# Three constants of a kernel's own planner, and sixteen small stores gathered into two

## The chip, the cores and the metric

The kernel runs on one core of one Trainium2 chip. The time is device microseconds of one execution; a kernel's time is the median over its runs. A core has TensorE (PE; its weight loads are listed as PEld), VectorE (DVE), ScalarE (ACT), GpSimd (POOL) and SyncE (SP), each with an instruction stream of its own that it works off in order, and 16 DMA engines that SP feeds here.

## The reference

One streaming step of a hybrid encoder layer, for 2048 frames of a new stream (the prompt) and 64 frames of a running one (the sample), width 1024, all in float32.

```python
h = rmsnorm(x, norm1_w)
proj = h @ w_in                       # q,k,v (3 x 512), z (512), a, b (4 each), u_pool (512)
qkv, conv_new = causal_short_conv(qkv_pre, conv_prev, conv_w)   # width 4; keeps the last 3 rows
...                                   # gated delta rule, 4 heads of 128, chunks; state S
o_pool, pool_new = multiscale_pool(u_pool, pool_prev, pos0, pool_w, pool_scale)  # keeps 15 rows
x = x + concat([o_delta, o_pool]) @ w_out
h = rmsnorm(x, norm2_w)
x = x + (silu(h @ w_gate) * (h @ w_up)) @ w_down                # 2816 wide
return rmsnorm(x, normf_w), conv_new, s_new, pool_new           # for prompt and sample
```

The histories that are returned are small: conv_new is 3 rows of 1536 channels, pool_new 15 rows of 512, for the prompt and again for the sample.

## The kernel before, in words

**The work.** Activations lie with channels on the partitions and frames along the free axis. Each float32 product is made of three matmuls in fp32r: weights and activations are split into a high part (a cast by ACT) and the rest (a subtraction by DVE), and high x high, high x rest and rest x high are summed in PSUM.

The *mixer* runs over four blocks of 512 frames; the first also holds the sample's 64. Per block: norm, input projection (21 weight tiles `win`), convolution, the delta rule (chains called Front and Head), pooling, output projection (`wout`). In the first block the split weights are stored to DRAM (`wnd`, and `wod` for the output projection, 512 KB each) and later blocks load them back (tile `wsp`). The output x2d goes to DRAM.

The *FFN* runs over three blocks of 704 frames in two halves of 352. `gate_up` makes one of 22 groups of 128 hidden channels with seven products of four tiles each, by a Strassen scheme: sums of weights (S1 to S4) times sums of activations (T1 to T4) are accumulated in three PSUM banks x, y and z. One product is 12 matmuls of 352 columns. In between, ACT and DVE copy or add what a bank holds so far (`g1`, `u2`, `g2`, in the trace g and u), and a later product accumulates into the same bank. The last one, weights 22 by T4 (px<-hBT,ws in the trace), goes into x after DVE has added x to u2. `down` (d in the trace) and `down_strassen` (dx, dy, dz) add the second matrix to y. The weight sums made in the first FFN block are stored (`gS`, 88 stores of 512 KB) and loaded again in the other two. Weight tiles go through rings: raw tiles (`wr...`), then split tiles (`ws...`); a place in a ring comes free when its last reader, a matmul or a store, is through.

**The planner.** The program doesn't issue instructions as it goes. The class `Machine` notes each one (`note`) with a cost (`cost`), a rank and its dependences, and at the end `issue` plays the whole program on five engines with modelled times and writes each engine's instructions in the order in which the play started them. On the chip each engine then keeps that order, and waits by semaphores where the real time differs. So the planner's numbers set no time; they decide the order only. In the play:

- an engine takes, of what is ready at that time, the instruction of the lowest rank. The rank is the program's order; some instructions get a lower one (`boost`). TensorE takes other kinds ahead of fp32r (`pick`).
- `done(p, q)` says when q may start after p: p's modelled end, plus a hand-over time `SYNC`, plus `MARGIN` of the engine q; where p or q is a DMA ("sync"), the margin is that of "sync". After a matmul it is MARGIN of q's engine.
- `run` keeps one time `wire` for all DMA traffic. A DMA takes 0.4 us of SP; the wire then takes its size at 400 bytes/ns over 300000 bytes and at 320 below, and it is taken to have landed 1.35 us after that. SP starts a transfer only when the wire's backlog is under 4 us, or, for one that is far ahead of TensorE, when there is none.
- a ring's place comes free at the modelled end of its last user (`t[3]` in `issue`), without a margin. The pool `f2` of the FFN comes free when every user of the mixer's pools (`cp1`, `gp`) has been played.
- a load's rank is that of its first user; a store's rank is its own place in the program.

**The histories.** In each block POOL copies the last 3 columns of the tile `ext` into `chist` and the last 15 of `pe` into `phist`, as the next block's history; at the mixer's end these are the prompt's results, and one store each (`cprompt`, `pprompt`) writes them. The sample is in the first block only; its last columns go out at once from `ext` and `pe`, 12 stores `csamp` and 4 stores `psamp`. At the mixer's end stand also `dprompt` and `dsamp`, the states.

Of the kernel before, what the change touches and what calls it, by code (L numbers as in the profile page):

```python
# [11 lines left out]
F32 = mybir.dt.float32  # L12
# [6 lines left out]
P = 128  # L19
# [3 lines left out]
DEC = 64  # L23
# [6 lines left out]
HP = 15  # L30
# [7 lines left out]
SO = PB[0] + 3  # L38
PSO = PB[0] + HP
# [19 lines left out]
class Machine:  # L59
# [234 lines left out]
    def run(self, op, t):  # L294
        op.start = t
        if op.eng == "tensor":

            free, kind = self.free["tensor"], op.kind
            if self.last == kind and op.ready <= free:
                op.start = max(t, self.at + op.ldw)  # L300
            elif kind == "r":
                if op.ready <= free:
                    op.start = max(op.ready, free - (0.028 if self.last == "h" else 0.081))
                op.occ, op.lat = op.occ + 0.087, op.lat + 0.087
            elif self.last == "h":
                op.occ, op.lat = op.occ + 0.054, op.lat + 0.054
            else:
                op.occ, op.lat = op.occ + 0.02, op.lat + 0.02
            self.at, self.last = op.start, kind
            self.free["tensor"] = op.start + op.occ  # L310
        elif op.eng == "sync":
            self.free["sync"] = t + op.occ
            self.wire = max(self.wire, t + op.occ) + op.size / (400e3 if op.size > 300000 else 320e3)
            op.lat = self.wire + 1.35 - t
        else:
            if op.port:

                other = "gpsimd" if op.eng == "vector" else "vector"
                more = min(max(self.busy[other] - t, 0.0), op.occ)
                op.occ, op.lat = op.occ + more, op.lat + more  # L320
                self.busy[op.eng] = t + op.occ
            self.free[op.eng] = t + op.occ

    def done(self, p, q):

        if p.eng == q.eng and p.eng != "sync":
            return p.start + (0.0 if p.eng == "tensor" else p.lat + self.OWN[p.eng] if id(p) in q.reads else p.occ)
        if p.eng == "tensor":
            return p.start + p.lat + MARGIN[q.eng]
        return p.start + p.lat + self.SYNC[q.eng] + MARGIN["sync" if p.eng == "sync" else q.eng]  # L330


class Engine:
# [20 lines left out]
def hybrid_kernel(ctx, tc, a, o):  # L354
    nc = machine = Machine(tc.nc)
# [71 lines left out]
    def pool(name, where=ctx, early=False, behind=False, **kw):  # L427
        return Pool(machine, where.enter_context(tc.tile_pool(name=name, bufs=1, **kw)), early, behind)
# [7 lines left out]
    cp1, gp = pool("cp1", p1, True), pool("gp", p1, True)  # L436
# [5 lines left out]
           "wout": dpool.tile([KT, 2, P, 1024], F32, tag="wod", name="wod")}  # L442
    gsd = {nm: dpool.tile([NF, P, 1024], F32, tag=f"g{nm}", name=f"g{nm}") for nm in KEEP}
    hpd = dpool.tile([NB2, 7, 4, P, N2], F32, tag="hpd", name="hpd")
# [16 lines left out]
    for lo, n in S0:  # L461
        for i in range(2):
            nc.sync.dma_start(out=x0[i][:, :, lo : lo + n],
                              in_=a["xT"][4 * i : 4 * i + 4, :, lo : lo + n].rearrange("k p t -> p k t"))
# [202 lines left out]
    def split(dst, sl, src):  # L667
        nc.scalar.copy(dst[:, 0, sl], src)
        tt(dst[:, 1, sl], src, dst[:, 0, sl].bitcast(F32), ALU.subtract)
# [101 lines left out]
    def evict(B, dst, pp, p, b, n):  # L771

        machine.boost = HURRY
        if B.j == 0:
# [71 lines left out]
    idbf = cp1.tile([P, P], BF16, tag="idbf", name="idbf")  # L846
    nc.vector.tensor_copy(idbf, ident)

    chist = cp1.tile([P, 12, 3], F32, tag="chist", name="chist")
    nc.vector.memset(chist, 0.0)  # L850
    phist = cp1.tile([P, 4, HP], F32, tag="phist", name="phist")
# [329 lines left out]
    def head_project(B, h, first=None):  # L1181

        j = B.j
        if len(heads) >= NY:
            drain(lambda: heads[-NY].done)
        Yqk = gp.tile([P, 2, 512], F32, tag="Yqk", name=f"Yqk{j}_{h}", bufs=NY)
        Yvz = gp.tile([P, 2, 512], F32, tag="Yvz", name=f"Yvz{j}_{h}", bufs=NY)
        Yi = [Yqk[:, 0], Yqk[:, 1], Yvz[:, 0], Yvz[:, 1]]
        hs = slice(h * DEC, (h + 1) * DEC)
        Si = [stash[i // 2][:, i % 2, hs] for i in range(4)]  # L1190
        for i in range(3):
            m = 4 * i + h
            ext = gp.tile([P, PX], F32, tag="ext", name=f"ext{j}_{m}", bufs=4)
            nc.gpsimd.tensor_copy(ext[:, 0:3], chist[:, m, :])
            if B.dec:
                nc.gpsimd.tensor_copy(ext[:, SO : SO + 3], schist[:, m, :])
            pp = first if first and i == 0 else project(B, 1 + 4 * h + i)
            for p, b, n, dst in B.segs:
                evict(B, ext[:, 3 + dst : 3 + dst + n], pp, p, b, n)
            nc.gpsimd.tensor_copy(chist[:, m, :], ext[:, B.PB : B.PB + 3])  # L1200
            if B.dec:
                nc.sync.dma_start(out=o["csamp"][m], in_=ext[:, SO + DEC : SO + DEC + 3])
            for y, lo, n in [(Yi[i], 0, B.PB)] + ([(Si[i], SO, DEC)] if B.dec else []):
                act(y, ext[:, lo : lo + n], AF.Copy, scale=convw[:, m, 0:1])
                for t in range(1, 4):
                    stt(y, ext[:, lo + t : lo + t + n], convw[:, m, t : t + 1], y, ALU.mult, ALU.add)
        pp = project(B, 4 + 4 * h)
        for p, b, n, dst in B.segs:
            evict(B, Yi[3][:, dst : dst + n] if dst < B.PB else Si[3], pp, p, b, n)
        for i, Yt in enumerate(Yi):  # L1210
            silu(Yt, f"{i}_{j}_{h}")
        out = [Head(f"p{j}_{h}_", B, h, Yqk, Yvz)]
        if B.dec and h == NH - 1:
            for i, Yt in enumerate(stash):
                silu(Yt.rearrange("p i n -> p (i n)"), f"s{i}")
            out.append(Head("s", B, None, *stash))
        return out

    def pool_group(B, g, pp):
        j, PW, win = B.j, B.PW, WIN[g]  # L1220
        pe = gp.tile([P, PX], F32, tag="ext", name=f"pe{j}_{g}", bufs=4)
        nc.gpsimd.tensor_copy(pe[:, 0:HP], phist[:, g, :])
        if B.dec:
            nc.gpsimd.tensor_copy(pe[:, PSO : PSO + HP], sphist[:, g, :])
        for p, b, n, dst in B.psegs:
            evict(B, pe[:, HP + dst : HP + dst + n], pp, p, b, n)
        nc.gpsimd.tensor_copy(phist[:, g, :], pe[:, B.PB : B.PB + HP])
        if B.dec:
            nc.sync.dma_start(out=o["psamp"][g], in_=pe[:, PSO + DEC : PSO + DEC + HP])
        cur, step = pe, 1  # L1230
        while step < win:
            nx = gp.tile([P, PX], F32, tag="pw", name=f"pw{j}_{g}_{step}", bufs=2)
            lo = 2 * step - 1
            nc.gpsimd.tensor_tensor(out=nx[:, lo:PW], in0=cur[:, lo:PW], in1=cur[:, lo - step : PW - step],
                                    op=ALU.add)
            cur, step = nx, 2 * step
        dd = gp.tile([P, PX], F32, tag="pw", name=f"pd{j}_{g}", bufs=2)
        stt(dd[:, HP:PW], cur[:, HP:PW], 1.0 / win, pe[:, HP:PW], ALU.mult, ALU.subtract)
        if j == 0:
            tt(dd[:, HP : HP + 16], cur[:, HP : HP + 16], pcnt[:, g, :], ALU.mult)  # L1240
            tt(dd[:, HP : HP + 16], dd[:, HP : HP + 16], pe[:, HP : HP + 16], ALU.subtract)
        yield 8.0
        if B.kept:
            nc.sync.dma_start(out=od[4 + g], in_=dd[:, HP:PW])
            return
        yield lambda: B.o is not None
        for s0, sn, dst in [(0, B.PB, 0)] + ([(B.PB, DEC, PSO)] if B.dec else []):
            split(B.o[4 + g], slice(s0, s0 + sn), dd[:, HP + dst : HP + dst + sn])
# [43 lines left out]
    def add_x(B, m, x, ps, lo):  # L1292
        machine.boost = HURRY
        tt(x, ps, x, ALU.add)
# [121 lines left out]
    for k in (4, 5, 6, 7, 0, 1, 2, 3):  # L1416
        t = wpool.tile([P, 512], F32, tag="xc", name=f"od{k}", bufs=XBUFS["xc"])
# [9 lines left out]
    drain(lambda: all(g.done for g in B.heads) and all(c.done for c in B.pools))  # L1427
    out_proj_last(B)
    drain()
    for nm, t in (("cprompt", chist), ("pprompt", phist)):  # L1430
        nc.sync.dma_start(out=o[nm].rearrange("m p t -> p m t"), in_=t)
    for nm, t in (("dprompt", Sp), ("dsamp", Ss)):
        nc.sync.dma_start(out=o[nm].rearrange("h k v -> k h v"), in_=t)
    p1.close()


    f2 = pool("f2", behind=True)
    wq["pool"] = f2
    banks += [("mm", PSM), ("bk", 1), ("mm", PSM), ("bo", 1), ("mm", PSM)] + [(f"b{i}", 1) for i in range(NLEV)]
    for nm in FH[3:]:  # L1440
        t = f2.tile([P, 4, 2, N2], F32R, tag=f"h{nm}", name=f"hB{nm}")
# [50 lines left out]
    def hurry(what, *args):  # L1492

        machine.boost = HURRY
        what(*args)
# [158 lines left out]
HOLD = 0.4, 3.0  # L1654
BACKLOG, IDLE, AHEAD_OPS = 4.0, 0.0, 400

MARGIN = {"tensor": 0.25, "vector": 0.1, "scalar": 0.1, "gpsimd": 0.1, "sync": 2.0}
NY, NLEV, NOUT, NX = 3, 3, 5, 3
XBUFS = {"xs": 4, "xc": 3}
LAT_A = 1.5  # L1660
# [10 lines left out]
ODB = 200  # L1671
PREPS = 1
HURRY = 400
KEEP = ("S1", "S2", "S3", "S4")
HOT_ROWS = BOOST
HPOOL = (0, 1, 2, 3)
# [113 lines left out]
```

## Time and profile before

| | us |
|---|---|
| median of 3 runs | 2397.7 (2396.79 to 2399.85) |
| the profiled execution, its time | 2395.04 |
| its span, first to last instruction | 2393.2 |
| TensorE busy | 2335.9 |
| DVE, ACT, POOL busy | 1770.8, 1295.0, 1000.6 |
| DMA | 471.38 MB, 58.4% of the 16 engines' span on SP's queue |
| granted TensorE clock, mean | 0.996 |

How to read the profile: a row of a group gives line, engine, operation, out<-in by the program's tile names, shape and count, then busy time in us, mean ns of one, and the idle time before it with what ended it. All instructions have line 278, since `issue` writes them; one goes by the tile names. A row of waits gives who waited for whom, us in total, times, and the longest. A row of the timeline gives start and length in us, then the instructions merged, and in brackets the idle time before and its releaser. A row of DMA issues gives count, KB each and the median us from issue to landing.

### The profile page before, as it was taken

How to read it: one execution, taken by the hardware profiler on the slowest of the kernel's cores; microseconds unless marked ns; L12 is line 12 of the kernel's file. 1: busy time of each engine (PE TensorE's matmuls, PEld its weight loads, DVE VectorE, ACT ScalarE, POOL GpSimd, SP SyncE). 2: the span in 40 equal slices, each digit the busy share in tenths (PEclk: the TensorE clock that was granted, in tenths of full speed). 3: DMA queues.
4: the chain of work that ended last, by engine and by line, in shares of the span. 5: the costliest groups of instructions: out<-in, count | busy, mean ns of one | idle time of the engine just before them, and what ended most of it. 6: DMA issues, size and time to landing. Idle time of an engine off the chain costs nothing.

```text
span 2393.2 us, 41899 instructions
## 1 busy us (share of the span) xinstructions
PE 2335.9 (98%) x14679; PEld 2175.2 (91%) x14679; DVE 1770.8 (74%) x3096; ACT 1295.0 (54%) x2920; POOL 1000.6 (42%) x1144
## 2 busy tenths in 40 slices
PE   8999999999999999999999999999999999999998
PEld 8898898878787868999999999999999999999998
DVE  8999875785677786887576765878777768777666
ACT  6766654573547464574354455653444564545444
POOL 3656542553357652354232234654322563223111
PEclk9999999999999999999999999999999999999999
DMA  8754465445555565877464566766654586454653
GB/s 286 241 164 164 137 235 201 166 157 184 176 196 180 169 211 170 303 277 272 171 212 149 177 215 214 254 209 201 240 173 142 162 297 215 142 174 159 200 177 104
DMA packets 219107, 471.38 MB, mean 197 GB/s; under 512 B 27408, under 2 KB 85776, under 8 KB 218896
## 3 DMA queue, kind: packets, MB, share of 16 engines
q1 hardware_dynamic: 218896, 468.71, 58.4%
q8 instruction: 115, 1.88, 0.3%
q14 instruction: 96, 0.79, 0.1%
HBM read 354.81 MB, written 113.80 MB: 196 GB/s over the span
## 4 chain that ended last, share of the span: by engine, by line
PE 75%; DVE 13%; ACT 4%; DMA 3%; issue 3%; POOL 1%; SPq 0%; DVEq 0%; POOLq 0%; ACTq 0%
PE px L278 16%; PE pp L278 15%; PE pz L278 10%; PE d L278 8%; PE py L278 7%; PE dx L278 5%; PE dy L278 3%; DVE hq L278 2%; PE pk_p L278 2%; PE pt_p L278 2%; PE dz L278 1%; ACT hr L278 1%; DVE hr L278 1%; DVE ws L278 1%; PE gr_p L278 1%
## 5 line engine op out<-in xcount | busy, mean ns | idle before, releaser
L278 PE MATMUL pp<-h,wsp 128*128 128x512 f32 (+1 forms) x2480 | 561.6, 367 | 12.8 <-DVE wsp L278 9.3
L278 PEld LDWEIGHTS pp<-h,wsp 128*128 128x128 f32 x2480 | 403.6, 191 | 60.6 <-ACT wsp L278 8.7
L278 POOL TENSOR_TENSOR Um_p<-Gst_p,lmask 128x256 f16<-128x256 f32 x224 | 180.3, 819 | 104.2 <-PE py_p L278 87.8
L278 ACT CAST ws<-wr 128x512 fp32r<-128x512 f32 x198 | 121.9, 618 | 164.0 <-PE d L278 47.0
L278 DVE TENSOR_TENSOR ws<-wr,ws 128x512 fp32r<-128x512 f32 x198 | 166.9, 846 | 47.7 <-ACT ws L278 42.9
L278 PE MATMUL pz<-op,wsp 128*128 128x288 f32 (+1 forms) x768 | 169.3, 357 | 2.8 <-ACT op L278 1.9
L278 PE MATMUL d<-h,wsd 128*128 128x352 f32 x1056 | 169.6, 322 | 0.5 <-ACT h L278 0.5
L278 PEld LDWEIGHTS d<-h,wsd 128*128 128x128 f32 x1056 | 168.5, 188 | 0.8 <-ACT h L278 0.8
L278 DVE TENSOR_TENSOR TV_p<-TV_p,pt_p 128x512 f16<-128x512 f16 x192 | 128.8, 680 | 31.7 <-PE pt_p L278 29.9
L278 PE MATMUL px<-hBT,ws 128*128 128x352 f32 x792 | 139.6, 325 | 10.4 <-DVE u L278 10.2
L278 POOL TENSOR_TENSOR wrS<-wr,wrS 128x512 f32<-128x512 f32 x44 | 64.0, 1454 | 193.1 <-DMA wrS<-in_wu_dram 66.6
L278 PE MATMUL px<-hBT,wsS 128*128 128x352 f32 x792 | 139.4, 324 | 5.1 <-ACT g L278 5.1
L278 PEld LDWEIGHTS px<-hBT,ws 128*128 128x128 f32 x792 | 127.7, 188 | 16.1 <-DVE u L278 16.1
L278 PE MATMUL px<-hA,ws 128*128 128x352 f32 x792 | 142.1, 322 | 0.3 <-DVE ws L278 0.2
L278 PE MATMUL py<-hB,wsS 128*128 128x352 f32 x792 | 141.9, 323 | 0.0
L278 POOL TENSOR_TENSOR q<-hr,hr 128x352 f32<-128x352 f32 x40 | 44.8, 1120 | 231.4 <-DVE hr L278 230.0
L278 PE MATMUL pz<-hB,ws 128*128 128x352 f32 x792 | 141.3, 322 | 0.0
L278 PE MATMUL px<-hA,wsS 128*128 128x352 f32 x792 | 138.0, 323 | 2.2 <-ACT g L278 2.1
L278 ACT ACTIVATE hr<-g 128x352 f32<-128x352 f32 x132 | 65.7, 498 | 135.9 <-DVE g L278 134.9
L278 PE MATMUL py<-hA,wsS 128*128 128x352 f32 x792 | 138.3, 322 | 0.0
L278 PEld LDWEIGHTS px<-hBT,wsS 128*128 128x128 f32 x792 | 129.3, 189 | 6.7 <-ACT g L278 6.5
L278 PEld LDWEIGHTS pz<-op,wsp 128*128 128x128 f32 x768 | 119.7, 189 | 14.3 <-ACT op L278 2.2
(670 smaller groups left out, 5841.6 us busy)
## 6 DMA issues: line engine op xcount, KB each, us to landing
wsS<-gS SPq DMA_DIRECT2D x176, 512.0 KB, 4.5
wsp<-wnd SPq DMA_DIRECT2D x126, 512.0 KB, 3.3
gS<-wsS SPq DMA_DIRECT2D x88, 512.0 KB, 4.3
wr<-in_wg_dram SPq DMA_DIRECT2D x132, 256.0 KB, 3.0
wnd<-wsp SPq DMA_DIRECT2D x42, 512.0 KB, 6.1
xd<-x2d SPq DMA_DIRECT2D x96, 176.0 KB, 3.4
wr<-in_wu_dram SPq DMA_DIRECT2D x66, 256.0 KB, 3.3
wrd<-in_wd_dram SPq DMA_DIRECT2D x56, 256.0 KB, 3.3
```

Of the source, the lines that this page charges most:

```text
L278: getattr(getattr(self.nc, op.eng), name)(*args, **kw)
```

## The change

Four edits. (1) `STORE`: in the play a store of more than 300000 bytes takes the wire at 300 bytes/ns and no longer at 400; loads stay at 400. (2) `MARGIN["sync"]` goes from 2.0 to 3.0 us: what waits for a DMA, and a DMA that waits for an engine, is played 1.0 us later. (3) `SLACK`: for a matmul noted after the mixer's end (`machine.second`), an input from ACT, DVE or POOL is played 0.6 us later. (4) The sample's histories are copied by POOL into two new tiles, `shist` and `sphst` (144 and 240 bytes a partition), and stored with the other results at the mixer's end: 2 stores for 16.

```diff
@@ run (class Machine)
             self.free["sync"] = t + op.occ
-            self.wire = max(self.wire, t + op.occ) + op.size / (400e3 if op.size > 300000 else 320e3)
+            self.wire = max(self.wire, t + op.occ) + op.size / (
+                (STORE if op.store else 400e3) if op.size > 300000 else 320e3)
             op.lat = self.wire + 1.35 - t
@@ done
         if p.eng == "tensor":
             return p.start + p.lat + MARGIN[q.eng]
-        return p.start + p.lat + self.SYNC[q.eng] + MARGIN["sync" if p.eng == "sync" else q.eng]
+        late = SLACK if q.eng == "tensor" and p.eng != "sync" and q.order > self.second else 0.0
+        return p.start + p.lat + self.SYNC[q.eng] + MARGIN["sync" if p.eng == "sync" else q.eng] + late
@@ hybrid_kernel
+    shist = cp1.tile([P, 12, 3], F32, tag="shist", name="shist")
+    sphst = cp1.tile([P, 4, HP], F32, tag="sphst", name="sphst")
@@ head_project
             if B.dec:
-                nc.sync.dma_start(out=o["csamp"][m], in_=ext[:, SO + DEC : SO + DEC + 3])
+                nc.gpsimd.tensor_copy(shist[:, m, :], ext[:, SO + DEC : SO + DEC + 3])
@@ pool_group
         if B.dec:
-            nc.sync.dma_start(out=o["psamp"][g], in_=pe[:, PSO + DEC : PSO + DEC + HP])
+            nc.gpsimd.tensor_copy(sphst[:, g, :], pe[:, PSO + DEC : PSO + DEC + HP])
@@ the mixer's end
-    for nm, t in (("cprompt", chist), ("pprompt", phist)):
+    for nm, t in (("cprompt", chist), ("pprompt", phist), ("csamp", shist), ("psamp", sphst)):
         nc.sync.dma_start(out=o[nm].rearrange("m p t -> p m t"), in_=t)
...
+    machine.second = len(machine.ops)
     f2 = pool("f2", behind=True)
@@ constants
-MARGIN = {"tensor": 0.25, "vector": 0.1, "scalar": 0.1, "gpsimd": 0.1, "sync": 2.0}
+MARGIN = {"tensor": 0.25, "vector": 0.1, "scalar": 0.1, "gpsimd": 0.1, "sync": 3.0}
...
+STORE = 300e3
+
+SLACK = 0.6
```

## The prediction

> **What bounds the kernel now.** I read the page's head first, then busy time by stage, then TensorE's waits, then the timeline at the waits that recur.
>
> ```profile
> span 2393.2 us, 41899 instructions
> PE 2335.9 (98%) x14679; PEld 2175.2 (91%) x14679; DVE 1770.8 (74%) x3096; ACT 1295.0 (54%) x2920; POOL 1000.6 (42%) x1144
> ...
> 0.00:60.00 60.00, 49.93 (x350) 48.72 (x351) 48.05 (x113) 37.36 (x86) 22.28 (x42) 1.00 0.86 286
> 60.00:240.00 180.00, 173.03 (x1356) 155.69 (x1355) 169.13 (x340) 125.24 (x330) 108.63 (x147) 0.99 0.58 190
> 240.00:980.00 740.00, 732.12 (x4472) 608.32 (x4471) 528.92 (x951) 412.83 (x1030) 347.19 (x457) 1.00 0.56 184
> 980.00:1430.00 450.00, 444.72 (x2755) 441.75 (x2754) 331.11 (x504) 235.57 (x476) 166.07 (x123) 1.00 0.62 219
> 1430.00:2340.00 910.00, 892.20 (x5492) 878.65 (x5491) 662.28 (x1135) 461.26 (x959) 344.71 (x365) 1.00 0.60 198
> 2340.00:2393.00 53.00, 43.90 (x264) 42.10 (x262) 31.27 (x57) 22.70 (x45) 11.72 (x12) 0.94 0.30 98
> ```
>
> TensorE is the bound: 2335.9 of 2393.2 us, so all that an order can win is 57.3 us. The rows by stage (length of the stretch, then busy PE, PEld, DVE, ACT, POOL, clock, DMA share, GB/s) place it: 10.1 us at the start, 7.0 in the rest of the first block, 7.9 in the rest of the mixer, 5.3 in the first third of the FFN, 17.8 in the rest, 9.1 at the end. Start and end are set by first loads and the last norm; the rest, 38.0 us, is what this change can reach. The waits by who ended them, first for the mixer (0 to 980), then 980 to 1430, then 1430 to 2340 (columns: total us, times, longest):
>
> ```profile
> PE pp L278 <- DVE wsp L278: 9.3, 2, 8.8
> PE gb_p L278 <- ACT ktl_p L278: 3.7, 4, 2.7
> PE pp L278 <- DMA wsp<-wnd: 1.7, 1, 1.7
> ...
> PE px L278 <- ACT g L278: 4.7, 5, 2.5
> ...
> PE px L278 <- DVE u L278: 10.2, 11, 1.6
> PE px L278 <- ACT g L278: 2.4, 3, 0.9
> PE dx L278 <- DVE y L278: 2.4, 3, 1.4
> PE dz L278 <- DVE y L278: 0.5, 1, 0.5
> PE dy L278 <- DVE y L278: 0.4, 1, 0.4
> ```
>
> The largest that is not the first load (8.8 of the 9.3) is px waiting for u, 11 times, 0.93 us on average. In gate_up the last product of a step, T4 by 22, accumulates into the bank that DVE reads when it adds x to u2. TensorE, at three such places (with the DVE rows of the second):
>
> ```profile
> 1494.85 0.64 PE L278 MATMUL px<-hA,ws 128*128 128x352 f32 x3
> 1496.07 2.20 PE L278 MATMUL px<-hBT,ws 128*128 128x352 f32 x12 [0.58 <-DVE u L278]
> 1498.11 1.61 PE L278 MATMUL px<-hA,ws 128*128 128x352 f32 x9
> ...
> 1737.73 0.81 PE L278 MATMUL dy<-hq,wsdS 128*128 128x352 f32 x4
> 1739.55 2.19 PE L278 MATMUL px<-hBT,ws 128*128 128x352 f32 x12 [1.02 <-DVE u L278]
> 1741.58 0.48 PE L278 MATMUL dy<-hq,wsdS 128*128 128x352 f32 x2
> ...
> 1737.84 1.22 DVE L278 TENSOR_TENSOR wsdS<-wrda,wsdS 128x512 fp32r<-128x512 f32 x1
> 1738.99 0.51 DVE L278 TENSOR_TENSOR u<-px,u 128x352 f32<-128x352 f32 x1
> ...
> 2280.46 0.80 PE L278 MATMUL dy<-hq,wsdS 128*128 128x352 f32 x4
> 2282.28 2.19 PE L278 MATMUL px<-hBT,ws 128*128 128x352 f32 x12 [1.02 <-DVE u L278]
> 2284.31 0.48 PE L278 MATMUL dy<-hq,wsdS 128*128 128x352 f32 x2
> ```
>
> These rows carry the forecast. Each time px cuts another product in two (3 matmuls, px, 9; or 4, px, 2). So the kernel's own planner ("the play": it writes each engine's order in advance) reckoned u ready at that moment, and put px there by its older rank, while other matmuls stood ready and are run right behind. The chip was about 1 us later than the plan: DVE took 1.22 us for one difference before u.
>
> **The change, part by part.** The planner's numbers make no instruction faster; they move instructions in their engine's order.
>
> *FFN results as later (SLACK, 0.6).* Every matmul noted after the mixer is now planned at least 0.6 us behind its ACT, DVE or POOL input. A matmul of 352 columns takes 0.16 us (1.92 us a dozen: px that waits lasts 2.19, its successor starts 2.03 after it), so where other matmuls are ready, three or four go ahead of px and the wait shrinks by 0.48 to 0.64. For u, with the middle of these: 11 x 0.56 = 6.2 us off the 10.2. What px delays, the product with u and the split of h, is late by 0.6 next; the down matmuls that need it come one gate_up step (7 x 1.92 = 13.4 us) later, so that is covered. The three waits for g after 1430 I take likewise: 3 x 0.56 = 1.7. The five for g before are another thing:
>
> ```profile
> 1015.49 2.08 PE L278 MATMUL pz<-hB,ws 128*128 128x352 f32 x12
> 1020.07 3.12 PE L278 MATMUL px<-hBT,wsS 128*128 128x352 f32 x12 [2.49 <-ACT g L278]
> ```
>
> Here px stands behind a whole product and cuts none, so the plan had g ready earlier; 0.6 more need not move it. I take 0 of the 4.7. The waits for y (3.3 us, 5 times) get 0.24 each, half of three matmuls, for want of a row that shows other work beside them: 1.2. Sum: -9.1. Against it stands that an order that is new everywhere has waits of its own; the best measure is what the present order left in the same stages, 23.1 us, of which 15.9 are addressed above (10.2, 2.4, 3.3) and 7.2 are of every other kind. I put +3.0, somewhat under half of these 7.2, for new ones (bounds 0 and +9.1, when all comes back). Net -6.1.
>
> *Long stores at 300 bytes/ns (STORE), loads as later (2.0 to 3.0).* What they bear on:
>
> ```profile
> wnd<-wsp SPq DMA_DIRECT2D x42, 512.0 KB, 6.1
> gS<-wsS SPq DMA_DIRECT2D x88, 512.0 KB, 4.3
> wod<-wsp SPq DMA_DIRECT2D x16, 512.0 KB, 4.3
> wsS<-gS SPq DMA_DIRECT2D x176, 512.0 KB, 4.5
> ...
> 59.94 0.62 ACT L278 CAST wsp<-wrp 128x512 fp32r<-128x512 f32 x1 [6.13 <-DMA wnd<-wsp]
> ...
> 64.11 0.39 PE L278 MATMUL gb_p<-Ghl,selp 128*128 128x256 f32 x1 [2.74 <-ACT ktl_p L278]
> ```
>
> 146 stores of 512 KB (42, 88, 16) are planned at 1.75 us on the wire for 1.31, 0.44 more each; a store of wnd lands after 6.1 us, where the plan's own sum (0.4 issue, 1.31, 1.35) said 3.06. A ring place of wsp comes back when its store lands; ACT's cast that waited 6.13 us for one held up ktl behind it and so TensorE by 2.74. With two stores ahead on the planned wire the cast moves 0.9 us back and others pass it: -0.9. That is one place; I put nothing for the rest. The 1.0 us on loads also holds for what feeds a DMA, so whole round trips through DRAM are planned up to 3 us longer, and on ACT and SP other work goes first. TensorE waited for a load itself only once (1.7 us), so little is to be had: 0, bounds -1.7 and, four such waits more, +6.8. The queue that is reordered is SP's; its loads of weights stand behind stores that wait for DVE, and whoever waits for those loads is ACT's and DVE's casts.
>
> *The sample's histories.* 16 stores leave SP's queue, 16 copies join POOL's, two stores join SP's:
>
> ```profile
> L278 SPq DMA_DIRECT2D out_csamp_dram<-ext x12: 383/427/2980, 38.2 to 166.9; - x12
>   ACT wsp L278: 0.6, 1
> out_psamp_dram<-pe SPq DMA_DIRECT2D x4, 7.5 KB, 1.6
> out_cprompt_dram<-chist SPq DMA_DIRECT2D x1, 18.0 KB, 6.7
> L278 POOL COPY chist<-ext x48: 181/190/720, 36.7 to 868.3; 128x3 f32<-128x3 f32 x48
> 290.47 0.43 SPq L278 DMA_DIRECT2D out_dsamp_dram<-consts  x1
> ```
>
> Removed: 16 issues of about 0.43 us, 6.9 us of SP over 200 us, and all that waited for them is ACT, once, 0.6. Added: 16 x 0.19 = 3.0 us on POOL, which is busy 109 of 180 there; the tile ext is held by a copy instead of a landing. The two gathered stores are noted at the mixer's end but nothing holds them there: dsamp, noted beside them, went out at 290 us, some 690 before the mixer ended. The one of csamp has cprompt's shape, 6.7 us to landing, beside weights that are loaded ahead. Bounds -0.6 and +3.0 (were DVE, busy 169 of 180 there, held for every copy). I take +0.5, nearest to the 0.6 of the only wait seen, with the sign of the load added.
>
> A rule speaks against this part: the Trainium skill, "SBUF — State Buffer", Who interferes with whom, says that a VectorE instruction with two SBUF inputs is blocked for the whole of a GpSimd instruction that reads SBUF. By this rule of the Trainium skill the estimate here is the upper end, +3.0, and the whole sum -4.0 in place of the -6.5 below. The trace agrees with it in that such a DVE instruction stretches (1.22 us for the difference above), but no row shows copies of 0.19 us doing so.
>
> **Sum**: -6.1 - 0.9 + 0 + 0.5 = -6.5. The profiled execution took 2395.0 us (span 2393.2 and 1.8 around it), so it would take 2388.5; the median of the runs is 2397.7, 2.7 above it, so the forecast there is 2391.2.
>
> **The rivals.**
> *It comes back elsewhere.* The new order wins the u waits and loses as much in waits for wsp, y and the fronts: for it, that DVE is busy 74% and 94% in the first block, so it is late wherever it is needed; against it, that the waits in the second half recur at the same place with the same length (1.02), which an added 0.6 answers directly. About 2397, from 2393 to 2401.
> *Slower: SP's order in the mixer.* Stores reckoned longer and data for stores 1 us later push loads of weights behind stores that in fact wait for DVE. Price: the wait of 1.7 us for wsp<-wnd, at each of the three block changes and once in the FFN, 6.8 us: 2397.7 + 6.8 = 2404.5 if what the FFN gains is lost with it, and 2398.0 if that stays. It decides from four such waits on. For it: DMA share 0.86 at the start and one such wait already. Against: only that one in 2393 us.
> *The full gain.* Nothing comes back (the +3.0 goes) and half of the g waits before 1430 and of the 7.9 us of the mixer go too: -6.5 - 3.0 - 2.4 - 4.0 = -15.9, 2381.8.
> *Copies hold DVE.* In the first block, where DVE is nearest to full, each of the 16 copies stops it for its 0.19 us and TensorE waits: +3.0 for +0.5, 2397.7 - 4.0 = 2393.7. It is what the rule of the Trainium skill named above would do.
>
> **How the numbers follow.** A difference below 0.2% (4.8 us) can't be told from none here. Forecast: 0.50; with the +3.0 at its bounds it is 2388.2 to 2397.3, and as the terms can be larger too I set it at 2386 to 2396. Comes back: 0.20. Slower order: 0.15. Full gain: 0.10. Copies hold DVE: 0.05. The time is the forecast's, 2391.2. Faster means below 2392.9: 0.42 of the forecast's 0.50 and all of the full gain, 0.52. Slower means above 2402.5: the slower order and 0.03 of the case where it comes back, 0.18. The same: 0.08 of the forecast, the copies' 0.05 and 0.17 of what comes back, 0.30. The range leaves out half of the full gain and a third of the slower order: 2381 to 2405.
>
> **What would show it.** Right: the group px<-hBT,ws waits about 4 us for u instead of 10.2, with px cutting its neighbour three or four matmuls later, the residue near 0.4 each; TensorE's busy time unchanged within 2 us; csamp's store one issue of 18 KB well before 400 us; no chist-like copy ahead of a TensorE wait. Wrong: u's total above 8; new waits of TensorE for wsp, ws or a DMA above 5 us; TensorE's busy time itself moved, because in the mixer other kinds of matmul now follow one another, a term that I hold at 0 since no row tells its direction; or the start longer than 10.1 us.

## The result and the profile after

The median went from 2397.24 us (4 runs, one more than at the prediction) to 2380.15 us (2379.02 to 2380.55, 4 runs): ratio 0.9933, interval 0.9921 to 0.9945, that is 17.1 us or 0.7% less. The forecast was 2391.2, 6.5 us less; the gain is 2.6 times that, and the result lies 0.9 us below the lower end of the stated range (2381). Ratios here and below are of executions at the full granted clock; the one other, the profiled execution of no_margin below, took 2835.81 us at a mean clock of 0.752 and leaves that kernel without a profile to read. The profiled execution of the changed kernel took 2379.8 us. The page's head after, and busy time by the same stretches of time as before:

```profile
span 2378.0 us, 41860 instructions
PE 2331.7 (98%) x14679; PEld 2176.7 (92%) x14679; DVE 1775.5 (75%) x3096; ACT 1288.2 (54%) x2920; POOL 1011.0 (43%) x1160
...
0.00:60.00 60.00, 49.76 (x349) 48.65 (x350) 48.87 (x116) 38.95 (x88) 23.04 (x46) 1.00 0.83 292
60.00:240.00 180.00, 176.34 (x1398) 160.66 (x1397) 169.63 (x351) 124.73 (x335) 117.91 (x162) 1.00 0.56 190
240.00:980.00 740.00, 731.33 (x4454) 609.44 (x4453) 535.87 (x949) 412.54 (x1032) 347.58 (x457) 1.00 0.57 187
980.00:1430.00 450.00, 445.70 (x2770) 442.93 (x2769) 329.97 (x499) 233.60 (x471) 164.66 (x122) 1.00 0.62 216
1430.00:2340.00 910.00, 899.70 (x5546) 887.58 (x5545) 667.15 (x1144) 464.05 (x969) 345.03 (x363) 1.00 0.61 199
```

The span fell by 15.2 us. TensorE's idle time fell from 57.3 to 46.3:

| stretch, us | idle before | idle after | change |
|---|---|---|---|
| 0 to 60 | 10.1 | 10.2 | +0.2 |
| 60 to 240 (first block) | 7.0 | 3.7 | -3.3 |
| 240 to 980 (rest of the mixer) | 7.9 | 8.7 | +0.8 |
| 980 to 1430 | 5.3 | 4.3 | -1.0 |
| 1430 to 2340 | 17.8 | 10.3 | -7.5 |
| the rest | 9.3 | 9.1 | -0.2 |

The stretches are of time, not of work: by 980 us the kernel after has started 6201 matmuls and the one before 6178, so it stands some 4 us further on in its work.

The other 4.2 us are busy time, of the same 14679 matmuls. Part of it is the clock. The granted clock fell to a half for 3.41 us three times in the middle of the execution before and twice after; the windows below hold exactly these (first three of before, then two of after; the seventh column is the clock):

```profile
65.27:68.68 3.41, 3.41 (x17) 3.27 (x16) 1.88 (x6) 3.12 (x11) 0.86 (x2) 0.50 0.29 107
253.00:256.42 3.42, 3.42 (x10) 2.76 (x10) 3.35 (x9) 2.14 (x6) 1.15 (x2) 0.50 0.22 63
1021.00:1024.42 3.42, 3.42 (x13) 3.42 (x13) 2.40 (x3) 3.39 (x8) 3.42 (x3) 0.50 0.77 243
...
806.46:809.87 3.41, 3.41 (x14) 2.96 (x12) 2.61 (x7) 0.00 (x0) 1.17 (x1) 0.50 0.55 193
864.49:867.90 3.41, 3.41 (x13) 2.41 (x12) 3.37 (x6) 1.14 (x2) 1.01 (x1) 0.50 0.76 146
```

One such window costs half of 3.41 us, 1.7 us, as an estimate: TensorE is busy through it at half its pace. That leaves 2.5 us of busy time without a cause that a run shows.

In the FFN the waits answer to those of before like this (980 to 2340; before: u 10.2 in 11, g 7.2 in 8), and the recurring place looks like this, TensorE and then DVE:

```profile
PE px L278 <- ACT g L278: 6.3, 16, 1.2
PE dx L278 <- DVE y L278: 1.7, 3, 0.6
PE px L278 <- DVE u L278: 1.4, 4, 0.6
PE dz L278 <- DVE y L278: 1.0, 3, 0.5
...
1722.03 2.08 PE L278 MATMUL px<-hA,wsS 128*128 128x352 f32 x12
...
1726.09 2.20 PE L278 MATMUL px<-hBT,wsS 128*128 128x352 f32 x12 [0.21 <-ACT g L278]
...
1730.21 0.48 PE L278 MATMUL dz<-hq,wsd 128*128 128x352 f32 x2
1730.53 2.08 PE L278 MATMUL px<-hBT,ws 128*128 128x352 f32 x12
...
1729.31 0.51 DVE L278 TENSOR_TENSOR u<-px,u 128x352 f32<-128x352 f32 x1
```

The last product still cuts a neighbour (dz, 2 then 4), but now it finds u done.

### The profile page after: what moved, and what is told of

Its sections match the earlier page's. It is cut to its first block, busy times and chain, and to the rows that moved or that the text cites. A ratio compares the mean times of both kernels' runs of the same rounds, so it can differ in the third digit from the quotient of the medians.

```text
span 2378.0 us, 41860 instructions
## 1 busy us (share of the span) xinstructions
PE 2331.7 (98%) x14679; PEld 2176.7 (92%) x14679; DVE 1775.5 (75%) x3096; ACT 1288.2 (54%) x2920; POOL 1011.0 (43%) x1160
## 5 line engine op out<-in xcount | busy, mean ns | idle before, releaser
L278 PE MATMUL pp<-h,wsp 128*128 128x512 f32 (+1 forms) x2480 | 560.6, 366 | 10.3 <-DVE wsp L278 9.8
```

The lines of the kernel that those rows point to most:

```text
L278: getattr(getattr(self.nc, op.eng), name)(*args, **kw)
```

## The experiments

Theories: (1) SLACK wins the u waits in the FFN, and the mixer moves little; (2) the DMA numbers or the histories mend a place of the mixer; (3) the order before is one draw among many, and any shift of the mixer's order gives a few us. Four kernels make one part of the change each, four leave one out, four go elsewhere. Times are medians; the ratios are to the kernel before, timed beside them on the same chip.

| run | parts | us | before | ratio, interval |
|---|---|---|---|---|
| only_slack | SLACK | 2387.50 | 2397.55 | 0.9960 (0.9946 to 0.9975) |
| only_margin | margin 3.0 | 2392.33 | 2397.55 | 0.9981 (0.9971 to 0.9990) |
| only_store | store 300 | 2383.68 | 2397.55 | 0.9945 (0.9930 to 0.9959) |
| only_hist | histories | 2387.19 | 2397.55 | 0.9964 (0.9951 to 0.9977) |
| no_slack | all but SLACK | 2389.57 | 2397.00 | 0.9972 (0.9962 to 0.9981) |
| no_store | all but store | 2383.98 | 2397.00 | 0.9951 (0.9935 to 0.9967) |
| no_margin | all but margin | 2377.57 | 2397.00 | 0.9926 (0.9907 to 0.9945) |
| no_hist | all but histories | 2383.01 | 2397.00 | 0.9948 (0.9930 to 0.9967) |
| store_500 | store 500 alone | 2389.81 | 2397.76 | 0.9966 (0.9953 to 0.9979) |
| margin_15 | margin 1.5 alone | 2401.75 | 2397.76 | 1.0019 (1.0010 to 1.0029) |
| store_slack | store 300, SLACK | 2381.11 | 2397.76 | 0.9926 (0.9911 to 0.9940) |
| slack_10 | all, SLACK 1.0 | 2383.43 | 2397.76 | 0.9938 (0.9922 to 0.9955) |

Differences of 2.6 to 3.8 us between two of these kernels, which come up below, stand between overlapping intervals: each is a hint of its sign and no more.

### SLACK alone, and all but SLACK

```diff
# only_slack, on the kernel before:
-        return p.start + p.lat + self.SYNC[q.eng] + MARGIN["sync" if p.eng == "sync" else q.eng]
+        return p.start + p.lat + self.SYNC[q.eng] + MARGIN["sync" if p.eng == "sync" else q.eng] + (
+            SLACK if q.eng == "tensor" and p.eng != "sync" and q.order > self.second else 0.0)
# no_slack, on the changed kernel:
-SLACK = 0.6
+SLACK = 0.0
```

> The kernel before with SLACK = 0.6 alone: the order differs only around and after the mixer's end. If the FFN's late results are what was won (first theory): -8 to -10 us, TensorE's wait for u from 10.2 to about 1.5 us and the mixer up to 980 us as before. If the new order gives it back (rival): -3 us or less, with u gone and waits for g, y and ws larger by as much.

> The changed kernel with SLACK = 0. First theory (the FFN's late results are a term of their own, 8 to 10 us): 2388 to 2390 us, with TensorE's wait for u back at about 10 us and the mixer as in the changed kernel. If the gains of the four parts overlap wholly (alone they gave 10.1, 5.2, 13.9 and 10.4 us, together 17): 2380 to 2384 us.

Waits of TensorE (980 to 2340 for only_slack, the whole for no_slack) and the stretches, first only_slack, then no_slack:

```profile
PE px L278 <- ACT g L278: 5.4, 18, 0.7
PE px L278 <- DVE u L278: 2.3, 2, 2.1
60.00:240.00 180.00, 172.22 (x1352) 155.10 (x1351) 169.65 (x340) 125.26 (x330) 108.53 (x147) 0.99 0.58 190
1430.00:2340.00 910.00, 897.88 (x5515) 884.53 (x5514) 667.76 (x1138) 459.07 (x962) 345.71 (x362) 1.00 0.60 198
```

```profile
PE px L278 <- DVE u L278: 11.4, 13, 1.6
1430.00:2340.00 910.00, 892.30 (x5480) 878.22 (x5479) 665.99 (x1133) 460.15 (x959) 341.51 (x361) 1.00 0.60 197
```

Alone SLACK gave -10.1 us, with u down from 10.2 to 2.3 and the first block as it was (7.8 idle for 7.0). Taken out of the whole it cost 9.4, and u was back at 11.4. The first theory holds for this part: from 1430 to 2340 TensorE idles 10.3 to 12.1 us in the five profiled kernels with SLACK 0.6, and 17.7 to 18.9 in the seven without.

### Store rate alone, all but the store rate, and the rate the other way

```diff
# only_store (300e3) and store_500 (500e3), on the kernel before:
-            self.wire = max(self.wire, t + op.occ) + op.size / (400e3 if op.size > 300000 else 320e3)
+            self.wire = max(self.wire, t + op.occ) + op.size / (
+                (300e3 if op.store else 400e3) if op.size > 300000 else 320e3)
# no_store, on the changed kernel:
-STORE = 300e3
+STORE = 400e3
```

> The kernel before with long stores at 300 bytes/ns alone. By the prediction's step -0.9 us, that is within 2 us of before, with ACT's 6.13 us wait for the store of wnd at 60 us shorter. If stores carry the mixer's gain: -3 to -6 us, with the 2.74 us wait of TensorE for ktl gone. u stays at about 10 us.

> The changed kernel with long stores at 400 bytes/ns. If the store rate is worth the 13.9 us that it gave alone: about 2394 us. If margin, histories and store rate mend the same stretch of the mixer (60 to 440 us), and one is enough: 2379 to 2383 us. If the mixer's time is a chance of the order: anything from 2374 to 2388 us, and lower than the changed kernel as easily as higher.

> The kernel before with long stores planned at 500 bytes/ns, away from the change's direction. If a later store in the plan is what gained (300 alone: -13.9 us): no gain, 2397 to 2402 us. If the order before is merely an unlucky one and any shift of it helps: faster by 4 to 10 us, about 2390 us.

only_store (stretches, then ACT and TensorE at the place that the prediction named), then store_500:

```profile
60.00:240.00 180.00, 174.03 (x1378) 158.35 (x1378) 170.20 (x347) 124.29 (x332) 109.38 (x147) 0.99 0.60 189
240.00:980.00 740.00, 734.74 (x4482) 610.47 (x4481) 532.08 (x948) 415.26 (x1037) 348.26 (x459) 1.00 0.56 187
...
60.43 0.62 ACT L278 CAST wsp<-wrp 128x512 fp32r<-128x512 f32 x1 [6.29 <-DMA wnd<-wsp]
...
64.07 0.39 PE L278 MATMUL gb_p<-Ghl,selp 128*128 128x256 f32 x1 [3.31 <-ACT ktl_p L278]
```

```profile
240.00:980.00 740.00, 731.33 (x4469) 606.41 (x4468) 532.35 (x954) 413.14 (x1031) 350.51 (x461) 1.00 0.56 185
```

The largest single gain, -13.9, and not where the prediction had it: the wait for the store of wnd is still there, 6.29 us, and TensorE's behind it 3.31. The rest of the mixer idles 5.3 us for 7.9. Of the 11.0 us by which the profiled span is shorter than before, 4.8 are busy time (2331.1 us), with three windows of half clock as before, so the clock is not their cause. The rate moved the other way gains as well, -8.0, though there the rest of the mixer idles 8.7 us and u is waited for 11.7; and with the other parts present the rate is worth 3.8 at most (2383.98 for 2380.15, with overlapping intervals). A gain on both sides of 400 that shrinks beside other edits is what the third theory says; that a truer rate gained was not shown.

### The margin of a DMA

```diff
# only_margin (3.0) and margin_15 (1.5), on the kernel before; no_margin (2.0), on the changed kernel:
-MARGIN = {"tensor": 0.25, "vector": 0.1, "scalar": 0.1, "gpsimd": 0.1, "sync": 2.0}
+MARGIN = {"tensor": 0.25, "vector": 0.1, "scalar": 0.1, "gpsimd": 0.1, "sync": 3.0}
```

> The kernel before with the DMA margin at 3.0 alone. If the 5.8 us that the mixer won come from transfers played later: -4 to -7 us, most of it before 980 us. If the mixer's gain comes from the histories, or is a chance of the order: within 3 us of before, either way. In the FFN u stays at about 10 us.

> The kernel before with the DMA margin at 1.5, away from the change's direction. If playing transfers later is what gained (3.0 alone: -5.2 us): no gain, 2397 to 2402 us. If any shift of the order helps: faster by 4 to 10 us, about 2390 us.

> The changed kernel with the DMA margin at 2.0. If the margin is worth the 5.2 us that it gave alone: about 2385 us. If the three parts mend the same stretch: 2379 to 2383 us. If the mixer's time is a chance of the order: 2374 to 2388 us, on either side of the changed kernel.

only_margin, then margin_15:

```profile
60.00:240.00 180.00, 174.38 (x1388) 158.61 (x1387) 167.97 (x346) 123.61 (x333) 108.83 (x147) 1.00 0.59 189
240.00:980.00 740.00, 730.35 (x4448) 607.73 (x4447) 535.96 (x950) 412.02 (x1032) 347.55 (x459) 1.00 0.57 186
...
61.99 0.39 PE L278 MATMUL gb_p<-Ghl,selp 128*128 128x256 f32 x1 [0.63 <-ACT ktl_p L278]
```

```profile
240.00:980.00 740.00, 726.61 (x4430) 602.81 (x4429) 532.04 (x950) 411.36 (x1030) 340.74 (x455) 0.99 0.55 183
```

Alone the margin goes one way: 4.0 us slower at 1.5, 5.2 faster at 3.0, where TensorE's wait for ktl at 60 us is 0.63 and no longer 2.74; at 1.5 the rest of the mixer idles 13.4 us for 7.9. At 3.0 the mixer as a whole did not gain idle time, against the expectation: the first block idles 5.6 us for 7.0, but the rest of the mixer 9.7 for 7.9, and up to 980 us both kernels idle 24.9. And in company the margin gives nothing: without it the changed kernel took 2377.57 (2376.95 to 2379.66 in the four other runs), the lowest median of all. Its interval overlaps that of the change (0.9907 to 0.9945 beside 0.9921 to 0.9945), so it isn't shown to be the better one.

### The histories alone, and all but the histories

```diff
# only_hist, on the kernel before (and its stores at the mixer's end); no_hist is the changed kernel with the old lines:
-                nc.sync.dma_start(out=o["csamp"][m], in_=ext[:, SO + DEC : SO + DEC + 3])
+                nc.gpsimd.tensor_copy(shist[:, m, :], ext[:, SO + DEC : SO + DEC + 3])
...
-            nc.sync.dma_start(out=o["psamp"][g], in_=pe[:, PSO + DEC : PSO + DEC + HP])
+            nc.gpsimd.tensor_copy(sphst[:, g, :], pe[:, PSO + DEC : PSO + DEC + HP])
```

> The kernel before with the sample's histories gathered alone. By the prediction +0.5 us, that is within 2 us of before. If copies on POOL hold DVE: +2 to +3 us, all before 240 us. If the 16 stores had delayed loads on SP's queue: -3 to -5 us, before 240 us. u stays at about 10 us.

> The changed kernel with the sample's histories stored one by one as before. If the histories are worth the 10.4 us that they gave alone: about 2390 us. If the three parts mend the same stretch: 2379 to 2383 us. If the copies on POOL cost: 2377 us. If the mixer's time is a chance of the order: 2374 to 2388 us, on either side.

only_hist (first block, landing of the wnd stores, and the place at 60 us), then no_hist, then SP's queue ahead of that place, before and in only_hist:

```profile
60.00:240.00 180.00, 177.31 (x1401) 160.68 (x1400) 171.14 (x352) 125.30 (x336) 112.64 (x162) 1.00 0.57 192
wnd<-wsp SPq DMA_DIRECT2D x42, 512.0 KB, 5.2
...
57.55 0.62 ACT L278 CAST wsp<-wrp 128x512 fp32r<-128x512 f32 x1 [3.95 <-DMA wnd<-wsp]
...
61.76 0.38 PE L278 MATMUL gb_p<-Ghl,selp 128*128 128x256 f32 x1 [0.53 <-ACT ktl_p L278]
```

```profile
60.00:240.00 180.00, 174.48 (x1390) 159.70 (x1389) 171.80 (x347) 123.64 (x330) 108.36 (x150) 1.00 0.58 191
wnd<-wsp SPq DMA_DIRECT2D x42, 512.0 KB, 5.8
```

```profile
53.42 0.42 SPq L278 DMA_DIRECT2D wnd<-wsp  x1
53.89 0.42 SPq L278 DMA_DIRECT2D out_csamp_dram<-ext  x1
54.36 1.08 SPq L278 DMA_DIRECT2D wnd<-wsp  x1
...
53.22 0.90 SPq L278 DMA_DIRECT2D wnd<-wsp  x2
```

Alone -10.4 us, taken out of the whole +2.9 (overlapping intervals). The first block's idle time falls from 7.0 to 2.7, where the prediction had +0.5 for the whole part: the stores of wnd land after 5.2 us at the median and no longer after 6.1, ACT's cast waits 3.95 us and no longer 6.13, and TensorE waits 0.53 for ktl and no longer 2.74. In no_hist the small stores are back, the landing is 5.8 and the first block idles 5.5. The median over all 42 stores moves by itself too (5.7 in only_slack, whose mixer is that of before), but the place at 60 us is plain. The store of wnd that ACT's cast waits for there was issued at 53.42 us, 0.47 ahead of a small store, and landed after 6.4 us; in only_hist it went out at 53.22 with no small store beside it and landed after 4.2. In the seven profiled kernels with a small store between these two stores of wnd, the first landed after 6.4 to 7.5 us and the second after 6.9 to 7.2; in the five with gathered histories after 4.2 to 4.4 and 5.0 to 5.2. Why so small a store holds its neighbours up that long is not shown. The first block idles 2.7 to 4.8 us in the five kernels with gathered histories and 5.2 to 7.8 in the eight without. So the effect on that block is shown; that all of the 10.4 comes from it is not: the orders differ everywhere behind it, and the profiled execution, the slowest of five (2391.09), is only 3.9 us shorter than that of before.

### Two more: store rate with SLACK, and a larger SLACK

```diff
# store_slack: only_slack and only_store together.  slack_10, on the changed kernel:
-SLACK = 0.6
+SLACK = 1.0
```

> The kernel before with the store rate at 300 and SLACK at 0.6, margin and histories as before. If the two gains add (13.9 and 10.1): 2373.5 us, faster than the changed kernel. If the store rate's gain is one draw of the order, which SLACK in the FFN does not touch: also 2372 to 2376 us, since the mixer's order stays that of the run with the store rate alone. If its gain lay in the FFN and SLACK replaces it: 2378 to 2382 us.

> The changed kernel with SLACK at 1.0 for 0.6. If what is left of TensorE's waits for g and u (6.3 and 1.4 us) shrinks with the slack: -2 to -5 us, 2375 to 2378 us, with g below 3 us. If 0.6 already takes what other work can cover: within 2 us of the changed kernel.

store_slack, then slack_10 (the waits of 980 to 2340):

```profile
1430.00:2340.00 910.00, 898.67 (x5522) 886.66 (x5521) 670.33 (x1143) 460.61 (x964) 340.40 (x357) 1.00 0.60 197
```

```profile
PE px L278 <- DVE u L278: 7.6, 7, 1.7
PE px L278 <- ACT g L278: 2.2, 5, 0.7
1430.00:2340.00 910.00, 894.29 (x5528) 884.95 (x5527) 660.22 (x1139) 464.08 (x968) 344.13 (x362) 1.00 0.61 199
```

Together the two edits gave -16.6, not the sum of -24.0. The time lies in the range of the third case, but its reason is not seen: from 1430 to 2340 only_store idles as long as the kernel before (17.9 us for 17.8), and store_slack 11.3, as elsewhere with SLACK; the rest of the mixer stays at 4.7. Against only_store some of it is lost in the first 60 us (1.0), from 980 to 1430 (1.2), at the end (0.7) and in busy time (1.6, with four windows of half clock for three). So the gains didn't add in full, and no single place accounts for it. SLACK at 1.0 is 3.3 us behind 0.6 (overlapping intervals): g shrinks as expected, but u is back at 7.6. More slack isn't shown to take more; it makes another order.

## Where the prediction was right, and which of its steps failed

The direction was right, and so was the mechanism of SLACK, which gave more than half of the gain. Everything else had been put at -0.4 us together and came to about 7 to 8; that it fell on the same side was not foreseen, and so luck.

**SLACK** was forecast at -6.1 net and is worth 9.4 to 10.1 (2.6 on top of the store rate alone, where the intervals overlap). The mechanism is the one named: other matmuls stood ready, and px went behind them. Two sizes were off. The u waits fell by 8.8, not 6.2, since the slack acts twice in a row in one step: on T3 by S3 (px<-hBT,wsS), the product ahead of u, and on the last one behind u. Before, at the place of the prediction's second rows, the product T3 by S3 started 3.52 us after T2 by S2, and after, 4.06 (0.21 of it a wait):

```profile
1730.51 2.08 PE L278 MATMUL px<-hA,wsS 128*128 128x352 f32 x12
...
1734.03 2.09 PE L278 MATMUL px<-hBT,wsS 128*128 128x352 f32 x12
```

The last product keeps its distance from it (4.44 us; before, 5.52 with 1.02 of waiting). While T3 by S3 starts later, DVE works off more of what stands ahead of u: u starts 3.2 us after that product's start, where it was 5.0. This is so at all of the places: in the kernel before, T3 by S3 started less than 3.6 us after T2 by S2 (two products take 3.84) in 19 of the 66 steps, and all 11 waits for u stand in these 19; in the kernel after, no step is below 3.6. Without SLACK (no_slack) it is 19 steps again, with 12 of the 13 waits. The residue of 0.4 each, forecast with one slack in mind, did not stay. And the price came as small waits for g, 16 of 0.39 us for 8 of 0.89, with 0.8 less in sum; the waits for y fell by 0.6, half of the 1.2 put. What is neither u, g nor y of the idle time from 980 to 2340 went from 23.1 - 20.7 = 2.4 to 14.6 - 10.5 = 4.1 us: +1.7. The prediction put +3.0 for new waits of every kind.

**The store rate** was put at -0.9, through ACT's wait of 6.13 us. That step is wrong: the wait is still there at 300, and TensorE's behind it is longer. The place was mended by the histories, and with the margin at 3.0 as well: there ACT's cast no longer stands ahead of ktl (in only_margin ACT waits 4.48 us for DVE's Yqk instead). What the rate gives it gives through another order, it seems, at 500 too.

**The histories** were put at +0.5. This is the term whose sign was wrong. The step that failed counted what waited for the small stores and SP's issue time, and left out what shares the wire with them: the 512 KB stores of wnd just ahead of them and behind them, for whose landing ACT and so TensorE wait (4.2 us without a small store beside it, 6.4 with one). The gathered store itself went as said, at 168 us (the kernel after):

```profile
L278 POOL COPY shist<-ext x12: 183/186/727, 37.0 to 168.2; 128x3 f32<-128x3 f32 x12
L278 SPq DMA_DIRECT2D out_csamp_dram<-shist x1: 388/388/388, 168.4 to 168.4; - x1
```

**The mixer** as a whole was given -0.4, with "comes back", "slower order" and "full gain" around it; the first block gave 3.3 and the clock 1.7, by the estimate above. The full gain at 2381.8 was the nearest of the rivals, though by other terms. The slower order did not come: no wait of TensorE for a DMA is left in the list of waits. The copies on POOL did not hold DVE so that it showed: the first block, for which the prediction had +3.0 at most by the rule of the Trainium skill ("SBUF — State Buffer", Who interferes with whom), became faster, and DVE's busy time there rose by 0.5 us in the changed kernel and by 2.0 in only_hist, with 11 and 12 instructions more in the stretch. Where copy and DVE met in the changed kernel, the copy was the one that lasted longer: four of the sixteen took 0.59 to 0.73 us and the rest 0.18 to 0.20, while DVE's differences of wsp beside a copy took 0.67 to 0.68, as they do beside no POOL work (0.68).

**TensorE's busy time** was held at 0, and a change of more than 2 us was one of the prediction's own signs of being wrong. It fell by 4.2 us, of which the clock is 1.7. In the twelve kernels with a profile to read beside that of before it is 2327.7 to 2339.0 us for the same 14679 matmuls. So it is a term of an order's price that the prediction lacked; what makes it stays open.

**The order as a draw**, which the prediction had only as "comes back elsewhere", is what the runs add. The four parts alone gave 10.1, 5.2, 13.9 and 10.4 us, 39.6 in sum, and together 17.1. Nine other orders of the mixer were timed, six without SLACK beside the kernel before and three with it beside only_slack: eight were faster by the median, margin_15 slower. Open stay how much of each part's gain in the mixer would survive another shift, and the 2.5 us of busy time.

## What to carry to other kernels

In a kernel whose order comes from a planner, a margin pays where the trace shows the bound engine waiting at one recurring place with other work ready behind it; count what the margin does to every step of that chain, not only to the last. A single trial of any other planner constant tells little: move it both ways, and look whether the stretch that it should act on moved. A small store is priced by the large transfers that go out just ahead of it and behind it, not by its own issue.

## What the runs showed of the hardware

A short gap can cost twice. Each window of half clock listed above began within 2 us of the end of a gap of TensorE that was itself shorter than 3.4 us: 2.74, 1.12 and 2.49 us before (the first and the third stand in the prediction), 2.00 and 1.92 after. The first two rows are of the kernel before, and no window followed the second:

```profile
251.14 1.06 PE L278 MATMUL pc<-consts,Rt 128*128 128x12 f32 x8 [1.12 <-DVE Rt L278]
...
1608.19 2.20 PE L278 MATMUL px<-hBT,ws 128*128 128x352 f32 x12 [1.56 <-DVE u L278]
...
805.99 0.27 PE L278 MATMUL pt_p<-Yt_p,TV_p 128*128 128x128 f16 x2 [2.00 <-ACT Yt_p L278]
...
862.76 0.27 PE L278 MATMUL py_p<-TV_p,Um_p 128*128 128x128 f16 x2 [1.92 <-DVE TV_p L278]
```

Behind the shortest stand eight matmuls of 12 columns. Most short gaps cost nothing more: between 20 and 2330 us the kernel before has 16 of 0.9 us and longer, and a window followed three; 1.73, 1.56 and 1.50 us stayed without. What decides is not shown. The Trainium skill, "TensorE: Matmul & The Clock Gate", The HAM clock gate, has the clock fall after an idle window of about 3.4 us; here gaps of 1.12 to 2.74 us were enough in these five cases, and the 1.7 us that a window costs is as much as such a gap itself. Between 1 and 4 such windows, two of them 6.8 us long, stood in the profiled executions that are read here, so a few us between two single executions may be the clock alone.
